# Twelve more k pairs in seven block products in the two SwiGLU FFNs of a decoder trunk

## The chip, the cores and the metric

The kernel runs on one core of one Trainium2 chip. The metric is the device time of one execution in microseconds (us). Beside it there is a trace of one profiled execution, with the start and the length of each instruction on each engine: TensorE (PE, with its weight loads as PEld), VectorE (DVE), ScalarE (ACT), GpSimd (POOL), and SyncE (SP), which issues most of the DMAs.

## The reference

The reference is a trunk of two decoder layers, each a mixer and a SwiGLU FFN, on 256 tokens of width 2048 in float32. Everything is matrix products over large weights with small work between them. The change is in the FFN:

```python
def swiglu(xn, w_gate, w_up, w_down):
    return (jax.nn.silu(xn @ w_gate) * (xn @ w_up)) @ w_down
...
        h = h + swiglu(rms_norm(h, norm_ffn[layer]), w_gate[layer], w_up[layer], w_down[layer])
```

w_gate and w_up are 2048 x 5632, w_down is 5632 x 2048, for each of the two layers.

## The kernel before, in words

**Split products.** TensorE takes fp32 data here in the reduced type fp32r. So each operand is split in two such parts, hi and lo: ScalarE casts raw to hi (L177), VectorE writes lo = raw - hi (L178). A product is then three matmuls, hi by hi, hi by lo and lo by hi (`three`, L508 to L511), each 128x128 by 128x512. Activations are split once and stay in SBUF: xh and xl for the input of gate and up, mh and ml for the input of down. Weights are split as they arrive, 512 KB at a time: a tile `raw` of 128x2x512, which is two k tiles of 128 rows (a k pair) by 512 columns. There are six buffers each for a weight's hi and lo and four for raw.

**Plain pairs and mixed pairs.** `pair_group` (L516 and on) computes a 2x2 arrangement of results at once: two weight matrices (gate and up columns, or two column blocks of down) by two blocks of 128 tokens (t0, t1). For a k pair it has two ways. A *plain* pair does all eight block products, 8 x 3 = 24 matmuls, into four PSUM banks (`plain`, "acc" in the trace); it needs two 1024-wide splits. A *mixed* pair does the 2x2 block product by the Strassen-Winograd scheme with seven products, 7 x 3 = 21 matmuls: four of them go to four further banks (`prods`), three to the plain ones. For that VectorE makes four 512-wide differences of the raw weights (L568 to L571), two of them in a tile t4 and two in place in raw. ScalarE and VectorE split these as ht and lt (two buffers each, so one mixed pair's worth), and the up weight's second k tile as a 512-wide hi and lo. Of the activations, four sums per pair are needed, made ahead of time by `sums_of` (L253 to L266) and kept split in sx (gate and up) and sd (down).

**Closing a group.** `combine` (L523 to L531) copies the first product bank to a tile c on ScalarE and adds the others on VectorE, with four 512-wide additions. Then gate/up groups add the four plain banks (L619), apply Silu (L621), multiply by the up half and the norm factor (L623), and turn the result to [hidden, token] by DMA transposes. The turned tile is joined and split into mh and ml (and the sums for down) some pairs later, inside the next group (`join`, after the position MID = 6, or MID_DOWN = 5 in a down group). Down groups add c to the residual h with four 512-wide additions (L708) and then the plain banks (`add_out`, L353).

**The order of the work.** An FFN has eleven gate/up groups of 512 hidden columns, in three parts PARTS = (0, 3, 7, 11): groups 0 to 2, 3 to 6, and 7 to 10. After each part follow two down groups over that part's hidden rows (12, 16 and 16 k tiles; in layer 1's last part the second is done with plain products alone). Which pairs are mixed, and in what order, is a list of (kind, pair) with kind 1 for mixed:

```python
ORDER = ((0, 0), (1, 1), (0, 2), (1, 3), (0, 4), (1, 5), (0, 6), (0, 7))
DOWN = {
    6: ((0, 0), (1, 1), (0, 2), (1, 3), (0, 4), (0, 5)),
    8: ((0, 0), (1, 1), (0, 2), (1, 3), (0, 4), (1, 5), (0, 6), (0, 7)),
}
```

So a group over eight pairs has three mixed ones: 5 x 24 + 3 x 21 = 183 matmuls. The banks alternate: a group's products use the four banks that held the plain results of the group before it. Each engine's instruction order is fixed when the kernel is built, by a scheduler that interleaves the matmuls of neighbouring pairs; each engine then runs its list in order and waits on semaphores. Weight loads are issued from SP.

Of the kernel before, what the change touches and what calls it, by code (L numbers as in the profile page):

```python
# [17 lines left out]
P = 128  # L18
D = 2048
S = 256  # L20
# [15 lines left out]
ORDER = ((0, 0), (1, 1), (0, 2), (1, 3), (0, 4), (1, 5), (0, 6), (0, 7))  # L36
DOWN = {
# [35 lines left out]
def trunk(  # L73
# [179 lines left out]
    def sums_of(pool, sh, sl, copies, full=None, tags=("tmp", "tmp"), bufs=None, box=None):  # L253
# [9 lines left out]
        nc.vector.tensor_tensor(out=s[:, 1, :], in0=s[:, 0, :], in1=full[:, 0, 0, :], op=ALU.subtract)  # L263
        nc.vector.tensor_tensor(out=s[:, 2, :], in0=full[:, 0, 0, :], in1=full[:, 0, 1, :], op=ALU.subtract)
        nc.vector.tensor_tensor(out=s[:, 3, :], in0=full[:, 1, 0, :], in1=s[:, 1, :], op=ALU.subtract)
        split_plain(sh, sl, s)  # L266

    def split_scaled(idx, n, extra=None, joined=None):
        for half in range(2):
# [13 lines left out]
            if extra is not None and pair in mixed_of(ORDER):  # L283
                sh, sl, pool = extra
                j = mixed_of(ORDER).index(pair)

                def copies(full):
                    for i in range(2):
                        g = gT[:, idx * KT + 2 * pair + i : idx * KT + 2 * pair + i + 1]
                        nc.scalar.mul(full[:, i, :], pt[:, i, :, :].rearrange("p t q -> p (t q)"), g)  # L290

                sums_of(pool, sh[:, j, :, :], sl[:, j, :, :], copies)
# [200 lines left out]
    def out_proj(w, idx, key, extra):  # L493
        last, rest = KT - 4, []
        for n0 in (0, 2):
# [3 lines left out]
            for i in range(2):  # L499
# [3 lines left out]
                    (LATER[n0 + i], split_turned(idx, n0 + i, *scrap(extra[2], n0 + i), extra))  # L503
                )
                square_sum(key, n0 + i)
        return rest

# [8 lines left out]
    def pair_group(fp, par, lhs, sums, mats, order, todo=(), halves=None, inner=None, raws=None):  # L516
        plain = [[bank(par, "acc") for _ in range(NT)] for _ in range(2)]
        todo = list(todo)
# [13 lines left out]
        for pos, (kind, pair) in enumerate(order):  # L532
# [4 lines left out]
            if not kind:  # L537
# [4 lines left out]
                for m, (w, c0) in enumerate(mats):  # L542
                    hi, lo = load_chunk(w, k0, c0, NB)
                    run_due(todo, pos)
                    for i, t in walk:
# [4 lines left out]
                            pos == 0 and i == 0, last and i == CK - 1,  # L550
# [38 lines left out]
            three(plain[0][0], xb[:, t0], lb[:, t0], hg[:, 1, :], lg[:, 1, :], False, False)  # L589
            three(plain[1][0], sh[:, 3, :], sl[:, 3, :], hu[:, 1, :], lu[:, 1, :], False, False)  # L590
            three(prods[1], sh[:, 0, :], sl[:, 0, :], ht[0], lt[0], first, last)
            three(prods[2], sh[:, 2, :], sl[:, 2, :], ht[1], lt[1], first, last)
            three(prods[3], sh[:, 1, :], sl[:, 1, :], ht[2], lt[2], first, last)
            three(plain[0][1], xb[:, t1], lb[:, t1], ht[3], lt[3], False, False)
# [4 lines left out]
    def ffn(layer, fp, sx, sd, key, todo, idx_next=None, key_next=None, finish=None):  # L599
        r = rstd(key)  # L600

        def sums_x(pair):
            j = mixed_of(ORDER).index(pair)
            return sx[0][:, j, :, :], sx[1][:, j, :, :]

        for g0, g1 in zip(PARTS, PARTS[1:]):
            end = g1 == PARTS[-1]
            nk = 4 * (g1 - g0)
            order = DOWN[nk // 2]
            for g in range(g0, g1):  # L610
                par = (g1 - 1 - g) % 2
                plain, c = pair_group(
                    fp, par, x_of, sums_x, [(w_gate[layer], g * NB), (w_up[layer], g * NB)], ORDER, todo
                )
                todo = []
                for m in range(2):
                    for t in range(NT):
                        o = c[:, 2 * m + t, :]
                        nc.vector.tensor_tensor(out=o, in0=plain[m][t], in1=o, op=ALU.add)  # L619
                for t in range(NT):  # L620
                    nc.scalar.activation(c[:, t, :], c[:, t, :], AF.Silu, scale=r[:, t : t + 1])  # L621
                for t in range(NT):
                    nc.vector.scalar_tensor_tensor(  # L623
                        out=c[:, t, :], in0=c[:, 2 + t, :], scalar=r[:, t : t + 1], in1=c[:, t, :], op0=ALU.mult, op1=ALU.mult
# [24 lines left out]
                def join(c=c, turned=turned, g=g, g0=g0, order=order):  # L649
# [8 lines left out]
                    for half in range(2):  # L658
                        pair = 2 * (g - g0) + half
                        if pair in mixed_of(order):  # L660
# [3 lines left out]
                                sd[0][:, j, :, :],  # L664
                                sd[1][:, j, :, :],
# [6 lines left out]
            def sums_d(pair, order=order):  # L672
                j = mixed_of(order).index(pair)
                return sd[0][:, j, :, :], sd[1][:, j, :, :]
# [16 lines left out]
            for n0 in (0, 2):  # L691
# [20 lines left out]
    def close_layer(layer, w_out, idx, key, **rest):  # L712
        with tc.tile_pool(name=f"fp{layer}", bufs=2) as fp:
# [3 lines left out]
            todo = out_proj(w_out, idx, key, (*sx, fp))  # L717
            sd = [fp.tile([P, nd, 4, P], F32R, tag=f"sd{i}", name=f"sd{i}", bufs=1) for i in range(2)]
            ffn(layer, fp, sx, sd, key, todo, **rest)
# [22 lines left out]
    with tc.tile_pool(name="ev", bufs=1) as ev:  # L742
# [223 lines left out]
        with tc.tile_pool(name="mp", bufs=1) as mp:  # L966
            def sums_m(pair):
                j = mixed_of(MIXQ).index(pair)
                return sx[0][:, j, :, :], sx[1][:, j, :, :]
# [129 lines left out]
    with tc.tile_pool(name="od", bufs=1) as od:  # L1099
# [65 lines left out]
        def sums_x(pair):  # L1165
            j = mixed_of(MIX).index(pair)
            return sx[0][:, j, :, :], sx[1][:, j, :, :]
# [154 lines left out]
```

## Time and profile before

| | us |
|---|---|
| median of 3 runs | 2077.48 |
| lowest and highest | 2077.07, 2077.85 |
| span of the profiled execution | 2076.6 |
| FFN of layer 0 (in that span) | 322.9 to 1009.3 |
| FFN of layer 1 | 1380.7 to 2066.9 |
| TensorE busy | 2066.4 |
| VectorE busy | 1824.5 |
| ScalarE busy | 1374.7 |
| GpSimd busy | 41.7 |

The profiled execution's own time is that of its span, from its first to its last instruction; the median of the runs is 0.9 us above it. Rows of an engine's busy time count the instructions' durations, merged where they overlap. A matmul's duration (0.39 us in the trace) includes the pipeline behind it, so that the distance of two starts, and not the duration, tells what one costs. In the views of the profile, each row names the engine, the line of the kernel before, the operation, and "output <- inputs" by the program's names; "x4" counts instructions taken together.

### The profile page before, as it was taken

The numbers are of one execution on the slowest core, as the hardware profiler recorded it, in microseconds if no ns is written. First come the engines' busy times: TensorE is split into PE (matmuls) and PEld (weight loads), VectorE is DVE, ScalarE is ACT, GpSimd is POOL, SyncE is SP. The second block draws the span as 40 slices with busy tenths as digits, with TensorE's granted clock in tenths as the row PEclk, the third lists the DMA queues.
The fourth block names the chain that finished last, engine by engine and source line by source line (L and its number), as shares of the span: only waits on it lengthen the run. The fifth ranks groups of instructions, "written<-read, shape, count | busy, mean of one in ns | idle before, by whom it ended". The sixth has DMA issues, their size and how long they took to land.

```text
span 2076.6 us, 26994 instructions
## 1 busy us (share of the span) xinstructions
PE 2066.4 (100%) x9473; PEld 1715.0 (83%) x9473; DVE 1824.5 (88%) x2410; ACT 1374.7 (66%) x1736; POOL 41.7 (2%) x66
## 2 busy tenths in 40 slices
PE   9999999999999999999999999999999999999998
PEld 7878888888888888888888888888888888888887
DVE  6788769999999999999899778689999999999994
ACT  6777678765676656667676776687655667456763
POOL 1010000000000000000000001000000000000000
PEclk9999999999999999999999999999999999999999
DMA  8566577666566666666576866586665667666764
GB/s 292 172 213 188 190 247 236 203 217 206 189 230 223 205 210 205 220 212 204 185 215 204 235 193 184 156 283 220 206 205 200 213 206 234 203 202 213 220 197 138
DMA packets 309575, 434.87 MB, mean 209 GB/s; under 512 B 106412, under 2 KB 114624, under 8 KB 309312
## 3 DMA queue, kind: packets, MB, share of 16 engines
q1 hardware_dynamic: 307088, 426.27, 65.1%
q0 software_dynamic: 1632, 5.80, 0.8%
q8 instruction: 74, 1.21, 0.2%
q10 hardware_dynamic: 720, 1.09, 0.2%
q14 instruction: 61, 0.50, 0.1%
HBM read 408.68 MB, written 2.12 MB: 198 GB/s over the span
## 4 chain that ended last, share of the span: by engine, by line
PE 97%; DVE 1%; ACT 1%; DMA 1%; issue 1%; SPq 0%; POOLq 0%; POOL 0%; ACTq 0%; DVEq 0%
PE acc L510 21%; PE acc L509 21%; PE acc L511 21%; PE acc L213 5%; PE acc L212 5%; PE acc L214 5%; PE prod L509 5%; PE prod L510 5%; PE prod L511 5%; PE p L369 1%; PE po L470 1%; DMA raw<-in_w_in_odd_dram 0%; ACT s L403 0%; PE po L471 0%; DVE lo L178 0%
## 5 line engine op out<-in xcount | busy, mean ns | idle before, releaser
L177 ACT CAST hi<-raw 128x1024 fp32r<-128x1024 f32 (+3 forms) x656 | 664.8, 1028 | 440.2 <-PE acc L511 269.1
L178 DVE TENSOR_TENSOR lo<-raw,hi 128x1024 fp32r<-128x1024 f32 (+3 forms) x656 | 772.8, 1192 | 146.3 <-ACT hi L177 143.5
L510 PE MATMUL acc<-lo,xh 128*128 128x512 f32 x1254 | 488.6, 390 | 0.0
L509 PE MATMUL acc<-hi,xh 128*128 128x512 f32 x1254 | 485.9, 390 | 0.5 <-ACT hi L177 0.5
L511 PE MATMUL acc<-hi,xl 128*128 128x512 f32 x1254 | 484.8, 389 | 0.0
L510 PEld LDWEIGHTS acc<-lo,xh 128*128 128x128 f32 x1254 | 235.4, 188 | 49.4 <-DVE lo L178 0.6
L509 PEld LDWEIGHTS acc<-hi,xh 128*128 128x128 f32 x1254 | 235.2, 188 | 49.5 <-ACT hi L177 0.7
L511 PEld LDWEIGHTS acc<-hi,xl 128*128 128x128 f32 x1254 | 235.4, 188 | 48.8
L510 PE MATMUL acc<-lo,mh 128*128 128x512 f32 x437 | 169.7, 389 | 0.0
L511 PE MATMUL acc<-hi,ml 128*128 128x512 f32 x437 | 168.4, 389 | 0.0
L509 PE MATMUL acc<-hi,mh 128*128 128x512 f32 x437 | 167.9, 389 | 0.0
L339 ACT CAST hi<-raw 128x512 fp32r<-128x512 f32 x109 | 67.6, 620 | 89.4 <-PE acc L511 80.5
L213 PE MATMUL acc<-lo,mh 128*128 128x512 f32 (+1 forms) x322 | 126.3, 392 | 0.0
L212 PE MATMUL acc<-hi,mh 128*128 128x512 f32 (+1 forms) x322 | 125.8, 391 | 0.0
L214 PE MATMUL acc<-hi,ml 128*128 128x512 f32 (+1 forms) x322 | 123.7, 391 | 0.0
L340 DVE TENSOR_TENSOR lt<-t,ht 128x1024 fp32r<-128x1024 f32 x95 | 115.8, 1219 | 5.2 <-ACT ht L339 5.1
L339 ACT CAST ht<-t 128x1024 fp32r<-128x1024 f32 x95 | 99.9, 1051 | 30.7 <-PE prod L511 28.8
L339 ACT CAST ht<-raw 128x1024 fp32r<-128x1024 f32 x95 | 99.7, 1050 | 29.7 <-PE acc L511 15.0
L340 DVE TENSOR_TENSOR lt<-raw,ht 128x1024 fp32r<-128x1024 f32 x95 | 115.7, 1218 | 1.8 <-ACT ht L339 1.8
L213 PE MATMUL acc<-lo,xh 128*128 128x512 f32 (+3 forms) x288 | 99.8, 348 | 0.2 <-DVE lo L178 0.2
L214 PE MATMUL acc<-hi,xl 128*128 128x512 f32 (+3 forms) x288 | 98.1, 344 | 0.0
L212 PE MATMUL acc<-hi,xh 128*128 128x512 f32 (+3 forms) x288 | 95.9, 347 | 0.3
(363 smaller groups left out, 3448.0 us busy)
## 6 DMA issues: line engine op xcount, KB each, us to landing
raw<-in_w_gate_dram SPq DMA_DIRECT2D x176, 512.0 KB, 4.5
raw<-in_w_up_dram SPq DMA_DIRECT2D x176, 512.0 KB, 4.6
raw<-in_w_down_dram SPq DMA_DIRECT2D x176, 512.0 KB, 5.1
raw<-in_w_in_odd_dram SPq DMA_DIRECT2D x88, 512.0 KB, 4.9
raw<-in_w_in_even_dram SPq DMA_DIRECT2D x51, 512.0 KB, 5.0
raw<-in_w_out_even_dram SPq DMA_DIRECT2D x32, 512.0 KB, 5.1
raw<-in_w_out_odd_dram SPq DMA_DIRECT2D x32, 512.0 KB, 4.8
hr<-in_w_in_even_dram SPq DMA_DIRECT2D x12, 512.0 KB, 4.6
```

The costliest lines, as they stand in the source:

```text
L177: latest[0] = nc.scalar.copy(hi[:, k, 0:n], raw[:, k, 0:n])
L178: nc.vector.tensor_tensor(out=lo[:, k, 0:n], in0=raw[:, k, 0:n], in1=hi[:, k, 0:n].bitcast(F32), op=ALU.subtract)
L212: nc.tensor.matmul(o, ah[:, ts], hi, start=(k == 0), stop=False)
L213: nc.tensor.matmul(o, ah[:, ts], lo, start=False, stop=False)
L214: nc.tensor.matmul(o, al[:, ts], hi, start=False, stop=(k == k_all - 1 and cs.stop == n))
L339: nc.scalar.copy(dst_h, src)
L340: nc.vector.tensor_tensor(out=dst_l, in0=src, in1=dst_h.bitcast(F32), op=ALU.subtract)
L369: nc.tensor.matmul(pq[j % 2][:, j // 2, :], q_of(j, b), k_of(j)[:, 0:cols], start=True, stop=True)
L470: nc.tensor.matmul(po, v_of(j, 0), tt[:, j, 0:2, :].rearrange("p c q -> p (c q)"), start=True, stop=False)
L509: nc.tensor.matmul(o, ah, hi, start=start, stop=False)
L510: nc.tensor.matmul(o, ah, lo, start=False, stop=False)
L511: nc.tensor.matmul(o, al, hi, start=False, stop=stop)
```

## The change

Four gate/up groups of each layer (1, 4, 6, 8) and both down groups of the middle part take four mixed pairs instead of three, in a new order that starts with a mixed pair and alternates. The added mixed pair is number 7.

- Its four sums need room. Of x, three go to the t1 halves of xh and xl at the k tiles 2, 6 and 10, which nobody reads (a mixed pair's first k tile is read in its t0 half alone), and the fourth to a new tile x4. Of the middle part's hidden activations all four go to the t1 halves of mh and ml at the k tiles 2, 6, 10 and 14.
- The first matmul into a bank sets its start flag through a helper `fresh`, since a group can now begin with a mixed pair.
- `combine` does the last two additions as one of 128x2x512 (with the up and gate columns of c in a new order), and the additions to h in a down group become two of 128x1024, in every group of the FFN.
- The scratch space of the software DMA queue (POOL's) goes from 4096 to 2048, which makes SBUF room for x4.

In the built program there are 36 matmuls fewer, and VectorE has 2449 rows where it had 2410, ScalarE 1662 where it had 1628; POOL and SP have as many as before.

```diff
+HEAVY = ((1, 1), (0, 0), (1, 3), (0, 2), (1, 5), (0, 4), (1, 7), (0, 6))
+FOURTH = 7
+DENSE = (1, 4, 6, 8)
+DEEP = (3,)
...
-        split_plain(sh, sl, s)
+        if x4 is None:
+            split_plain(sh, sl, s)
+        else:
+            split_plain(sh, sl, s[:, 0:3, :])
+            split_plain(x4[:, 0, :], x4[:, 1, :], s[:, 3, :])
...
-            if extra is not None and pair in mixed_of(ORDER):
-                sh, sl, pool = extra
-                j = mixed_of(ORDER).index(pair)
+            if extra is not None and (pair in mixed_of(ORDER) or pair == FOURTH):
+                sh, sl, x4, pool = extra
...
+                if pair == FOURTH:
+                    sums_of(pool, rooms(xh), rooms(xl), copies, x4=x4)
+                else:
+                    j = mixed_of(ORDER).index(pair)
+                    sums_of(pool, sh[:, j, :, :], sl[:, j, :, :], copies)
...
+    def rooms(m):
+        return m[:, 2:11:4, P:S]
...
+        begun = set()
+
+        def fresh(*at):
+            known = at in begun
+            begun.add(at)
+            return not known
...
+            if halves is None:
+                nc.vector.tensor_tensor(out=c[:, 1, :], in0=prods[3], in1=c[:, 0, :], op=ALU.add)
+                nc.vector.tensor_tensor(out=c[:, 2, :], in0=prods[2], in1=c[:, 1, :], op=ALU.add)
+                nc.vector.tensor_tensor(
+                    out=c[:, 1:4:2, :],
+                    in0=prods[1].rearrange("p (a n) -> p a n", a=1).broadcast_to([P, 2, NB]),
+                    in1=c[:, 1:3, :],
+                    op=ALU.add,
+                )
+                return c
...
-                            pos == 0 and i == 0, last and i == CK - 1,
+                            fresh(m, t), last and i == CK - 1,
...
         def sums_x(pair):
+            if pair == FOURTH:
+                return [[m[:, k, P:S] for k in (2, 6, 10)] + [x4[:, a, :]] for a, m in enumerate((xh, xl))]
...
-            order = DOWN[nk // 2]
+            order = HEAVY if g0 in DEEP else DOWN[nk // 2]
             for g in range(g0, g1):
                 par = (g1 - 1 - g) % 2
                 plain, c = pair_group(
-                    fp, par, x_of, sums_x, [(w_gate[layer], g * NB), (w_up[layer], g * NB)], ORDER, todo
+                    fp,
+                    par,
+                    x_of,
+                    sums_x,
+                    [(w_gate[layer], g * NB), (w_up[layer], g * NB)],
+                    HEAVY if g in DENSE else ORDER,
+                    todo,
                 )
...
             def sums_d(pair, order=order):
+                if pair == FOURTH:
+                    return [[m[:, k, P:S] for k in (2, 6, 10, 14)] for m in (mh, ml)]
...
-                for m in range(2):
-                    for t in range(NT):
-                        o = h[:, t, (n0 + m) * NB : (n0 + m + 1) * NB]
-                        nc.vector.tensor_tensor(out=o, in0=c[:, 2 * m + t, :], in1=o, op=ALU.add)
+                for t in range(NT):
+                    o = h[:, t, n0 * NB : (n0 + 2) * NB]
+                    nc.vector.tensor_tensor(
+                        out=o, in0=c[:, 2 * t : 2 * t + 2, :].rearrange("p a n -> p (a n)"), in1=o, op=ALU.add
+                    )
...
-    nc = _bacc.Bacc("TRN2", target_bir_lowering=False, num_devices=1, dynamic_dma_scratch_size=4096)
+    nc = _bacc.Bacc("TRN2", target_bir_lowering=False, num_devices=1, dynamic_dma_scratch_size=2048)
```

More of the change, by code (lines that the diff above doesn't have):

```diff
@@ L506, in out_proj, with four @@
         return rest
+    def four(s, j):
+        return [s[:, j, e, :] for e in range(4)]
+    def rooms(m):
+        return m[:, 2:11:4, P:S]
     def three(o, ah, al, hi, lo, start, stop):
@@ L588, in pair_group @@
             three(prods[0], xa[:, t0], la[:, t0], hg[:, 0, :], lg[:, 0, :], first, last)
[L589 to L594, printed above, removed]
+            three(plain[0][0], xb[:, t0], lb[:, t0], hg[:, 1, :], lg[:, 1, :], fresh(0, 0), False)
+            three(plain[1][0], sh[3], sl[3], hu[:, 1, :], lu[:, 1, :], fresh(1, 0), False)
+            three(prods[1], sh[0], sl[0], ht[0], lt[0], first, last)
+            three(prods[2], sh[2], sl[2], ht[1], lt[1], first, last)
+            three(prods[3], sh[1], sl[1], ht[2], lt[2], first, last)
+            three(plain[0][1], xb[:, t1], lb[:, t1], ht[3], lt[3], fresh(0, 1), False)
         if inner is None:
@@ L663, in join @@
                                 fp,
-                                sd[0][:, j, :, :],
-                                sd[1][:, j, :, :],
+                                *[sums_m[:, j, :, :] if pair != FOURTH else m[:, 2:15:4, P:S] for sums_m, m in zip(sd, (mh, ml))],
                                 None,
```

31 lines of the change are left out of this document (18 added, 13 removed).

## The prediction, made before the changed kernel ran

> **What bounds the kernel now.** I read the profile in this order: busy shares, then stretches of the FFN as a table by stage, then the groups of VectorE's instructions in those stretches, then waits, then the timeline around one block-product pair. The first page says that TensorE is never without work, and that VectorE is the next engine:
>
> ```profile
> span 2076.6 us, 26994 instructions
> PE 2066.4 (100%) x9473; PEld 1715.0 (83%) x9473; DVE 1824.5 (88%) x2410; ACT 1374.7 (66%) x1736; POOL 41.7 (2%) x66
> ```
>
> 88% is a mean over stages. The change sits in the two FFNs, so I cut the trace there. The first fence holds both FFNs whole, the second four stretches of 41.5 us, one group each, of layer 0's middle part: gate/up groups 4, 5 and 6 and the first down group:
>
> ```profile
> 322.90:1009.30 686.40, 686.40 (x3037) 568.41 (x3036) 647.55 (x807) 448.85 (x508) 0.69 (x1) 1.00 0.65 208
> 1380.70:2066.90 686.20, 686.20 (x3033) 568.17 (x3032) 629.93 (x781) 433.64 (x484) 1.79 (x3) 1.00 0.64 205
> ```
>
> ```profile
> 552.20:593.70 41.50, 41.50 (x185) 34.37 (x184) 39.74 (x52) 28.30 (x31) 0.00 (x0) 1.00 0.66 218
> 593.70:635.20 41.50, 41.50 (x185) 34.37 (x184) 39.98 (x52) 28.68 (x32) 0.00 (x0) 1.00 0.66 217
> 635.20:676.70 41.50, 41.50 (x185) 34.37 (x184) 39.74 (x51) 28.47 (x31) 0.00 (x0) 1.00 0.67 215
> 676.70:718.20 41.50, 41.50 (x185) 34.37 (x184) 39.88 (x49) 26.91 (x28) 0.00 (x0) 1.00 0.67 216
> ```
>
> The columns are the stretch, its length, then busy time with count for PE, weight loads, DVE, ACT and POOL, the granted clock, and the DMA share with GB/s. PE is busy through all of both FFNs (686.40 of 686.40), so every matmul taken out is worth its full pitch, as long as nothing else becomes late. But DVE is busy for 39.7 to 40.0 of each 41.5 us. Only some 1.5 to 2.3 us per group are free there. DMA (0.65) and ACT (28 of 41.5) have room.
>
> A matmul's pitch, and DVE's and ACT's own spacing, come from starts that follow each other:
>
> ```profile
> 621.25 0.39 PE L510 MATMUL acc<-lo,sx 128*128 128x512 f32 x1
> 621.48 0.39 PE L511 MATMUL acc<-hi,sx 128*128 128x512 f32 x1
> 621.71 0.62 PE L509 MATMUL prod<-ht,sx 128*128 128x512 f32 x2
> 622.16 0.39 PE L510 MATMUL prod<-lt,sx 128*128 128x512 f32 x1
> ```
>
> ```profile
> 616.68 0.29 DVE L263 TENSOR_TENSOR s<-s,c 128x128 f32<-128x128 f32 x1
> 616.88 1.22 DVE L340 TENSOR_TENSOR lt<-t,ht 128x1024 fp32r<-128x1024 f32 x1
> ...
> 619.35 0.69 DVE L568 TENSOR_TENSOR t<-raw 128x512 f32<-128x512 f32 x1
> 619.95 0.69 DVE L569 TENSOR_TENSOR t<-raw 128x512 f32<-128x512 f32 x1
> 620.55 1.22 DVE L340 TENSOR_TENSOR lt<-raw,ht 128x1024 fp32r<-128x1024 f32 x1
> ...
> 622.29 4.63 DVE L178 TENSOR_TENSOR lo<-raw,hi 128x1024 fp32r<-128x1024 f32 x4
> 626.83 1.22 DVE L340 TENSOR_TENSOR lt<-t,ht 128x1024 fp32r<-128x1024 f32 x1
> ...
> 630.71 0.68 DVE L528 TENSOR_TENSOR c<-prod,c 128x512 f32<-128x512 f32 x1
> 631.31 0.68 DVE L529 TENSOR_TENSOR c<-prod,c 128x512 f32<-128x512 f32 x1
> 631.91 0.68 DVE L340 TENSOR_TENSOR lo<-raw,hi 128x512 fp32r<-128x512 f32 x1
> ```
>
> Four matmuls lie between 621.25 and 622.16: 0.2267 us each. Four 1024-wide DVE operations take (626.83 - 622.29)/4 = 1.135 us each, 512-wide ones 0.600 (619.35, 619.95, 620.55; from PSUM too: 630.71, 631.31, 631.91), 128-wide ones 0.20 (616.68 to 616.88). The durations are 0.085 longer than these intervals because the instructions overlap; I add intervals. The 512-wide scalar_tensor_tensor gets 0.746 - 0.085 = 0.66 (groups of DVE's instructions from 510.8 to 676.7 us; busy time, mean ns, idle time before):
>
> ```profile
> L178 DVE TENSOR_TENSOR lo<-raw,hi 128x1024 fp32r<-128x1024 f32 x52 | 62.5, 1220 | 5.1 <-ACT hi L177 5.0
> L340 DVE TENSOR_TENSOR lt<-t,ht 128x1024 fp32r<-128x1024 f32 x12 | 14.6, 1221 | 1.5 <-ACT ht L339 1.4
> L623 DVE SCALAR_TENSOR_TENSOR c<-c,r 128x512 f32<-128x512 f32 x6 | 4.2, 746 | 0.0
> ```
>
> **The change, part by part.** *TensorE.* A k pair taken as seven products issues 21 matmuls, as eight products 24. Twelve more pairs (two layers, each four gate/up groups and two down groups) remove 36 matmuls: 36 x 0.2267 = **-8.16 us**. The built order has exactly 36 fewer, and the order outside the FFNs is unchanged.
>
> *VectorE, one pair.* A plain pair is two 1024-wide subtractions (2.27 us). A mixed pair is three of them and five 512-wide operations: 3 x 1.135 + 5 x 0.600 = 6.40. So each turned pair adds **4.13 us on DVE and removes 0.68 us from PE**.
>
> *VectorE, one group.* Before, a gate/up group is 5 x 2.27 + 3 x 6.40 = 30.55 of pairs, 4 x 0.6 to combine, 4 x 0.6 for L619, 2 x 0.66 for L623, and 2.5 for the join of the turned tile (1.135 + four 128-wide + one 512-wide): 39.2 us against 183 x 0.2267 = 41.49 on PE. That agrees with the rows of 39.7 to 40.0 (whose ends count overlap). Spare: 2.3 us. The two merges are worth little: one 1024-wide instead of two 512-wide saves 1.200 - 1.135 = 0.065 us. After:
> - a dense gate/up group: 4 x 2.27 + 4 x 6.40 + 2.33 + 2.4 + 1.32 + 2.53 = 43.3 against 180 x 0.2267 = 40.81: **short by 2.5**;
> - the first down group of the middle part: 34.7 + 2.33 + 2.27 (h) + 2.4 (L353) + 2.53 = 44.2: short by 3.4;
> - the second (no join): 41.7: short by 0.9.
>
> Groups 1 and 4 stand between groups with 2.3 us to spare. But group 6 and both down groups follow each other: 2.5 + 3.4 + 0.9 = 6.8 us short in a row; then comes group 7, light, and group 8, short again.
>
> *Page against row.* The Trainium skill, in "VectorE: DVE Perf Modes", section "The TRN2 errata", gives the fp32 tensor_tensor add as (N+151)/0.96 ns: 0.691 us for 512, 1.224 for 1024. The trace agrees on single durations (0.69, 1.22). Adding such durations over a group of before (20 x 1.224 + 24 x 0.691 + 2 x 0.746 + 4 x 0.285) would make 43.7 us, and PE would stall by 2 us in each group; the rows show no stall, so the intervals decide.
>
> *How far DVE is ahead.* A shortage costs nothing until DVE's lead over PE is used up. The lead is limited by buffers: ht and lt have two tiles each, so the next pair's ht cast on ACT waits until PE has read the last one. What it is now, at a second mixed pair of a group:
>
> ```profile
> 615.40 1.05 ACT L339 CAST ht<-t 128x1024 fp32r<-128x1024 f32 x1
> ```
>
> The cast ends at 616.45, the lt subtraction quoted above at 616.88 + 1.22 = 618.10, and PE reads lt at 622.16: 4.1 us ahead. I take 5.0, somewhat in favour of the change.
>
> *The running sum.* In the built order of the changed kernel I start at the lt of group 6's second mixed pair with a lead of 5.0 and add up both engines to the L353 addition that frees the first bank for the second down group's products. DVE, after that lt: 41 operations of 1024, 51 of 512, two of L623, eight of 128: 41 x 1.135 + 51 x 0.6 + 2 x 0.66 + 8 x 0.2 = 80.1. PE, between the two readers: 311 matmuls, 70.5. So DVE ends 80.1 - 70.5 - 5.0 = **4.6 us** late, in each layer (layer 1 has the same sequence).
>
> This supposes that DVE never waits on the way. It must: the built order puts the lt products of group 6's second and third mixed pairs almost side by side on PE (only 12 matmuls between the last reader of the second's ht and the first reader of the third's lt). The third's ht cast can't start until that reader is done, so DVE, 5 us ahead, does its four subtractions (2.4) and then idles: 5.0 + 0.2 + 1.05 - 2.4, some 3.5 us. After it, the lead is 12 x 0.2267 - 1.05 - 1.22 = 0.4. From there to the same L353 addition DVE has 40 x 1.135 + 47 x 0.6 + 2 x 0.66 + 8 x 0.2 = 76.5 and PE 299 matmuls, 67.8: 76.5 - 67.8 - 0.4 = **8.3 us** late.
>
> Group 8: from its first mixed pair to its last DVE has 28.0 us (15 x 1.135 + 17 x 0.6 + 4 x 0.2) against 98 matmuls (22.2) and a lead of 5.0: 0.8, and up to 4.9 if DVE idles on ht as above. Groups 1 and 4: 0 to 1.2, with their neighbours' slack.
>
> *The small parts.* Three more sums of x, for pair 7 (four 128-wide, the splits, four scalings on ACT): +1.5 us on DVE ahead of group 0, covered by its 2.3 of slack; 0 to 1.5 per layer if not. ACT's extra work, two 1024 casts of 1.05 less half a cast, is 1.5 us per pair and goes into its 13 us of idle time per group. Fourth sums in unread halves need no new wait on a reader. No DMA is added on SP. The software queue's smaller ring touches POOL alone, outside the FFN (below).
>
> *Sum.* Per layer the least is 4.6 + 0.8 = 5.4, with idling 8.3 + 0.8 to 4.9 + 0 to 1.2 = 9.1 to 14.4. Both layers: 10.8 at least, 18 to 29 with idling. Less 8.16: +2.6 at least, **+10 to +21** with idling. I take the lower part, +13, because the ends of the idling sums use the lead at its smallest at each place. The profiled execution is 2076.6 and the runs are 0.9 above it (median 2077.5); the difference is added to the latter: **2090 us**.
>
> **Rivals.**
> 1. *The cover holds.* Over a whole FFN, DVE goes from 647.55 to 647.55 + 6 x 4.13 - 16 x 0.065 - 11 x 0.065 + 1.5, some 672, still below PE's 686.4 - 4.1 = 682.3. If DVE were free to run far ahead, its slack of 35 us would absorb everything: 2077.5 - 8.2 = **2069**. For it: six weight buffers (three pairs) let DVE split plain chunks earlier, and ACT mostly waits for PE (waits from 510.8 to 759.6 us: total, times, longest):
>
> ```profile
> ACT hi L177 <- PE acc L511: 51.7, 35, 4.2
> DVE lo L178 <- ACT hi L177: 8.0, 15, 1.1
> ```
>
> Against it: the same row says that the lead is already at its cap, so slack can't be saved up beyond it, and 6.8 us short in a row are more than 5. It decides from a lead of about 10 us at group 6.
> 2. *The shortage without idling*: +2.6, **2080**. For it: DVE's order has other splits to put into a gap; against it, that order is fixed when the kernel is built.
> 3. *Worse hand-overs.* With a mixed pair first, the products need the banks of the group before at once, where a plain pair's 24 matmuls (5.4 us) stood between. If each of the six dense groups per layer waits 1 to 2 us for L619 or L353: 2090 + 12 to 24 us, **above 2102**.
> 4. *The POOL queue.* With half the ring its DMAs wait for each other. The row that shows POOL waiting for such loads:
>
> ```profile
> POOL cb L1151 <- DMA cb<-scratch: 20.7, 4, 6.7
> ```
>
> Doubled, it would be 20.7 us more on POOL, of which nothing ended on PE before; at the outside +20, **2110**, with PE idle outside the FFNs.
> 5. *The change doesn't do what it says*: the built order has the 36 matmuls fewer and DVE's 48 further 512-wide subtractions, so I give this nothing.
>
> **How the numbers follow.** Forecast (shortage with idling, 2084 to 2102): 0.62. Rival 2 (2078 to 2083): 0.17. Rival 1 (2067 to 2073): 0.09. Rival 3: 0.08. Rival 4: 0.04. The range is 2078 to 2102: it leaves out rival 1, rival 3 and most of rival 4, about 0.2. A difference of 0.2% (4.2 us) is about what a measurement of this kernel can tell from none: faster 0.09, same 0.14 (rival 2 below 2081.6), slower 0.77.
>
> **What would show it.** In the changed profile: PE waits in the FFN for DVE's lt and lo and for c or h, where there were none; those waits concentrated from group 6's third mixed pair to the second down group, 6 to 9 us per layer, and a few us in group 8; DVE near 100% from group 6 to the down groups and a DVE wait on ACT's ht of about 3 us in group 6; 36 matmuls fewer at an unchanged pitch of 0.2267; no change outside the FFNs. I am wrong if PE stays gapless (rival 1), if the gaps are at the first products of the dense groups and wait for bank releases (rival 3), or if gaps appear outside the FFNs (rival 4).

## The result

The changed kernel takes **2151.0 us** (median of 4 runs, 2147.8 to 2151.9), the kernel before 2077.3, measured beside it: a ratio of 1.035, 95% interval 1.0337 to 1.0366. The forecast was 2090, with a range up to 2102. The sign was right, the size was not: +74 us, where +13 had been worked out. The profiled execution has a span of 2146.1.

First the busy times of the changed kernel, from the head of its profile:

```profile
span 2146.1 us, 26989 instructions
PE 2086.6 (97%) x9437; PEld 1707.8 (80%) x9437; DVE 1872.6 (87%) x2449; ACT 1394.3 (65%) x1770; POOL 43.8 (2%) x66
```

TensorE has 36 records fewer, as the change says, and VectorE 48 us more work (1824.5 to 1872.6). Yet VectorE's share fell, from 88% to 87%. It isn't busier; the span grew by more than its work. The stretches that answer to the two FFN rows of before, in the same columns:

```profile
323.00:1043.90 720.90, 697.58 (x3020) 564.99 (x3018) 669.27 (x825) 457.41 (x523) 0.69 (x1) 0.99 0.64 198
```

```profile
1419.30:2136.00 716.70, 695.49 (x3014) 562.62 (x3013) 653.26 (x803) 443.98 (x502) 1.75 (x3) 1.00 0.64 197
```

The FFNs grew by 34.5 us (686.4 to 720.9) and 30.5 us (686.2 to 716.7). Another 4.0 us lie between them, from the end of the one to the start of the other (1009.3 to 1380.7 before: 371.4; 1043.9 to 1419.3: 375.4). That is 69.0 of the 69.5 us by which the span grew, so nothing is lost elsewhere. TensorE now waits. The waits of the whole span, of which before had none over 1.2 us:

```profile
PE prod L526 <- ACT ht L350: 15.8, 13, 3.1
PE prod L527 <- DVE lt L351: 8.3, 9, 1.6
PE acc L527 <- DVE lo L182: 4.3, 6, 1.3
PE acc L526 <- ACT hi L181: 4.1, 6, 1.1
PE pt L283 <- DVE h L364: 3.7, 1, 3.7
```

The two largest are for the cast ht of a mixed pair and the split lt behind it, 24.1 of the 36.2 us shown. And VectorE, which was to be the bound, waits itself in the FFN of layer 0 (total, times, longest); the kernel before, then the changed one:

```profile
DVE lo L178 <- ACT hi L177: 22.3, 40, 1.5
DVE lt L340 <- ACT ht L339: 2.6, 5, 1.4
```

```profile
DVE lt L351 <- ACT ht L350: 15.5, 14, 3.3
DVE lo L182 <- ACT hi L181: 9.8, 16, 3.2
DVE lo L351 <- ACT hi L350: 7.9, 7, 1.8
DVE c L551 <- PE prod L528: 6.4, 3, 4.0
DVE t L602 <- DMA raw<-in_w_down_dram: 3.3, 2, 2.0
DVE t L602 <- DMA raw<-in_w_up_dram: 3.1, 4, 1.3
```

The waits for ht went from 2.6 to 15.5 us, and waits for weights appear where there were none. The waits for hi (L177, now L182) went the other way, from 22.3 to 9.8 us.

**By stretch.** The groups' limits follow from counting matmuls from the FFN's first one. From group 6 to the end of the middle part's down groups, before and in the change:

```profile
635.25:759.65 124.40, 124.40 (x550) 103.00 (x550) 118.99 (x147) 77.14 (x82) 0.00 (x0) 1.00 0.66 212
```

```profile
642.45:782.40 139.95, 128.97 (x542) 99.63 (x541) 126.26 (x155) 80.71 (x90) 0.00 (x0) 1.00 0.60 184
```

This stretch should be 2.0 us shorter (nine matmuls fewer) and is 15.6 us longer, so 17.6 us are lost. The whole FFN of layer 0, in us, with 0.68 us (three matmuls) for each dense group added to the growth:

| | before | change | lost | forecast |
|---|---|---|---|---|
| group 0 | 41.5 | 41.5 | 0.0 | 0 to 1.5 |
| groups 1 and 2, first part's down groups | 146.5 | 154.3 | 8.5 | 0 to 1.2, with group 4 |
| groups 3 to 5 | 124.5 | 123.8 | 0.0 | as above |
| group 6, middle part's down groups | 124.4 | 140.0 | 17.6 | 4.6 to 8.3 |
| groups 7 to 9 | 124.5 | 129.5 | 5.7 | 0.8 to 4.9 |
| group 10, last part's down groups | 125.2 | 132.0 | 6.8 | none |

The series that the forecast had worked out lost twice its upper figure, and more than half of the loss lies outside it.

**One place closely: group 6.** The timeline of ScalarE, then that of VectorE, in the changed kernel:

```profile
660.20 1.05 ACT L350 CAST ht<-t 128x1024 fp32r<-128x1024 f32 x1 [1.62 <-PE prod L528]
661.16 1.05 ACT L350 CAST ht<-raw 128x1024 fp32r<-128x1024 f32 x1
662.11 1.99 ACT L693 COPY c<-c 128x1024 uint16<-128x1024 uint16 x2
667.06 1.35 ACT L700 COPY c<-turned 128x1024 uint16<-128x1024 uint16 x1 [2.96 <-DMA turned<-c]
668.36 1.05 ACT L350 CAST ht<-t 128x1024 fp32r<-128x1024 f32 x1
```

```profile
665.49 0.69 DVE L605 TENSOR_TENSOR raw<-raw 128x512 f32<-128x512 f32 x1
669.45 1.23 DVE L351 TENSOR_TENSOR lt<-t,ht 128x1024 fp32r<-128x1024 f32 x1 [3.27 <-ACT ht L350]
671.01 0.29 DVE L266 TENSOR_TENSOR s<-c 128x128 f32<-128x128 f32 x1 [0.33 <-ACT c L700]
671.22 0.28 DVE L268 TENSOR_TENSOR s<-c 128x128 f32<-128x128 f32 x1
672.84 0.69 DVE L602 TENSOR_TENSOR t<-raw 128x512 f32<-128x512 f32 x1 [1.34 <-DMA raw<-in_w_up_dram]
```

ScalarE's join of group 5 (L700) waits 3 us for the turned tiles, and the next ht cast stands behind it in ScalarE's list. But that cast could hardly have come sooner. It overwrites one of the two ht tiles, and TensorE was still reading it; the last matmul that does so is this one:

```profile
667.94 0.39 PE L528 MATMUL prod<-ht,sx 128*128 128x512 f32 x1
```

It ends at 668.33, and the cast starts at 668.36. So VectorE's wait of 3.3 us for that cast is the one that the prediction had at this place, "some 3.5 us", and the join's wait lies inside it. What the prediction didn't have is the 1.3 us more for a weight. In the kernel before the same two copies came together, with no wait, 7.3 us after the 16-bit copies that feed the transposes:

```profile
644.25 1.99 ACT L646 COPY c<-c 128x1024 uint16<-128x1024 uint16 x2
...
653.50 2.58 ACT L653 COPY c<-turned 128x1024 uint16<-128x1024 uint16 x2
```

The chain of waits of the changed kernel from 662 to 690 us (start, length, piece) shows a third party, SyncE's queue:

```profile
662.21 1.90 ACT c L693 x2
664.11 0.27 SPq L695
664.42 1.26 SPq L695
...
665.78 1.21 SPq L695
...
667.03 1.26 SPq L695
...
668.40 4.36 DMA raw<-in_w_up_dram
...
672.84 0.69 DVE t L602
```

L695 issues the transposes, four of them, one after another on the queue that issues the weight loads too. The next weight load leaves behind them, 4.3 us after the copies that start them (664.11 to 668.40), and takes 4.4 us; VectorE stands at L602 until it lands. TensorE's two largest gaps in this group follow from it: 0.8 us at 673.45, for a cast of that weight, and 1.6 us at 675.53, for the lt that stands behind L602 in VectorE's list.

### The profile page after: what moved, and what is told of

Read it like the earlier page. It is cut to its first block, busy times and chain, and to the rows that moved or that the text cites. A ratio compares the mean times of both kernels' runs of the same rounds, so it can differ in the third digit from the quotient of the medians.

```text
span 2146.1 us, 26989 instructions
## 1 busy us (share of the span) xinstructions
PE 2086.6 (97%) x9437; PEld 1707.8 (80%) x9437; DVE 1872.6 (87%) x2449; ACT 1394.3 (65%) x1770; POOL 43.8 (2%) x66
## 4 chain that ended last, share of the span: by engine, by line
PE 75%; DVE 10%; DMA 5%; issue 4%; ACT 4%; SPq 2%; ACTq 0%; POOLq 0%; DVEq 0%; POOL 0%
PE acc L526 15%; PE acc L527 15%; PE acc L528 15%; PE acc L217 5%; PE acc L216 5%; PE acc L218 5%; PE prod L526 4%; PE prod L528 4%; PE prod L527 4%; DVE lo L182 3%; DMA raw<-in_w_down_dram 3%; DVE lt L351 2%; SPq L695 1%; DMA raw<-in_w_up_dram 1%; ACT hi L181 1%
## 5 line engine op out<-in xcount | busy, mean ns | idle before, releaser
L181 ACT CAST hi<-raw 128x1024 fp32r<-128x1024 f32 (+2 forms) x644 | 649.5, 1026 | 372.2 <-PE acc L528 220.7
L182 DVE TENSOR_TENSOR lo<-raw,hi 128x1024 fp32r<-128x1024 f32 (+2 forms) x644 | 756.5, 1189 | 119.6 <-ACT hi L181 116.6
L527 PE MATMUL acc<-lo,xh 128*128 128x512 f32 x1198 | 467.8, 390 | 0.0
L528 PE MATMUL acc<-hi,xl 128*128 128x512 f32 x1198 | 464.2, 390 | 0.0
L526 PE MATMUL acc<-hi,xh 128*128 128x512 f32 x1198 | 460.5, 391 | 3.8 <-ACT hi L181 2.3
L350 ACT CAST ht<-t 128x1024 fp32r<-128x1024 f32 x107 | 112.4, 1051 | 108.8 <-PE prod L528 78.7
L351 DVE TENSOR_TENSOR lt<-t,ht 128x1024 fp32r<-128x1024 f32 x107 | 130.4, 1219 | 33.7 <-ACT ht L350 32.7
L351 DVE TENSOR_TENSOR lt<-raw,ht 128x1024 fp32r<-128x1024 f32 x107 | 130.2, 1216 | 0.8 <-ACT ht L350 0.4
L217 PE MATMUL acc<-lo,mh 128*128 128x512 f32 (+1 forms) x322 | 126.3, 392 | 0.0
L350 ACT CAST ht<-raw 128x1024 fp32r<-128x1024 f32 x107 | 112.1, 1048 | 8.3 <-DVE raw L605 6.2
L526 PEld LDWEIGHTS acc<-hi,mh 128*128 128x128 f32 x413 | 78.4, 190 | 26.6 <-ACT hi L181 4.0
```

The costliest lines, as they stand in the source:

```text
L181: latest[0] = nc.scalar.copy(hi[:, k, 0:n], raw[:, k, 0:n])
L182: nc.vector.tensor_tensor(out=lo[:, k, 0:n], in0=raw[:, k, 0:n], in1=hi[:, k, 0:n].bitcast(F32), op=ALU.subtract)
L217: nc.tensor.matmul(o, ah[:, ts], lo, start=False, stop=False)
L350: nc.scalar.copy(dst_h, src)
L351: nc.vector.tensor_tensor(out=dst_l, in0=src, in1=dst_h.bitcast(F32), op=ALU.subtract)
L526: nc.tensor.matmul(o, ah, hi, start=start, stop=False)
```

## The experiments

Each is the changed kernel with the edit shown, unless it says otherwise. Three theories were held against each other first: A, VectorE's own work; B, waits that pass from queue to queue in the built order; C, the merged additions.

**Parts of the change: e1 to e3, and its order: e4.**

```diff
e1  DENSE = ()               DEEP = ()
e2  DENSE = (1, 4, 6, 8)     DEEP = ()
e3  DENSE = ()               DEEP = (3,)
e4  HEAVY = ((0, 0), (1, 1), (0, 2), (1, 3), (0, 4), (1, 5), (1, 7), (0, 6))
```

> No group has a fourth mixed pair (DENSE and DEEP empty); the merged additions in c and h, the sums of pair 7 and the smaller queue space stay, and TensorE has the matmul count of before. Three theories are held against each other. Theory A (throughput: VectorE simply has too much to do in the dense groups): 2076 to 2079, no TensorE gaps in the FFNs. Theory B (order: with the dense groups the built order closes the group before late, and waits pass from one engine's queue to the next): the same, 2076 to 2079. Theory C (the merged additions and the new layout of c hold the down groups of the first and last part up, where gaps of 5 to 8 us per layer were seen although they got no fourth pair): about 2077 + 2 x (5 to 8) + 2 x (5 to 7) = 2097 to 2107.

> Only the gate/up groups 1, 4, 6 and 8 have a fourth mixed pair (8 groups, 24 matmuls fewer, -5.4 us); the down groups are as before. Theory A: each dense group is short by 2.5 us and stands beside groups with 2.3 us to spare and a lead of some 5 us, so nothing or little is lost: 2072 to 2078. Theory B: the gaps at groups 1 and 8 and a part of those at group 6 stay, and so do the gaps in the down groups of the first and last part: 2077 - 5.4 + 2 x (4 + 5 + 6 + 6 + 7) = about 2120, at least 2095.

> Only the two down groups of the middle part have a fourth mixed pair (4 groups, 12 matmuls fewer, -2.7 us). Theory A: short by 3.4 + 0.9 us in a row with a lead of about 5: 2074 to 2080. Theory B: a part of the gaps between group 6 and the second down group stays, 5 to 12 us per layer, and nothing elsewhere: 2085 to 2099.

> The whole change, but the dense order begins with a plain pair and has the mixed pairs 1, 3, 5, 7 behind it: (0,0), (1,1), (0,2), (1,3), (0,4), (1,5), (1,7), (0,6). Work on each engine is unchanged to the instruction, only its order moves. Theory A: as the change, 2140 to 2155. Theory B: the plain pair in front lets the group before close in time, and much of the loss goes: 2090 to 2125.

Measured: e1 2081.1 (ratio 1.0015, 1.0006 to 1.0025), e2 2114.2 (1.018), e3 2090.6 (1.006), e4 2147.3 (1.034), before 2077.8. C falls: the merges, together with pair 7's sums and the smaller ring, cost 3.3 us, not 20. A, as I had sized it, falls with e2: e2, with four dense groups per layer, takes 36.4 us more than before, where A allowed none. e2 and e3 also show that the parts don't add up: over e1 they lose 33.1 and 9.5, together 42.6; the whole change loses 69.9 over e1. B falls in one form with e4, since a plain pair in front changes nothing.

**Single dense groups: e9, e10.**

```diff
e9   DENSE = (4, 8)   DEEP = ()   the 512-wide additions of before
e10  DENSE = (6,)     DEEP = ()
```

> Only gate/up groups 4 and 8 have a fourth pair (4 groups, 12 matmuls fewer, -2.7 us), down groups as before, 512-wide additions as before. In the run with all four dense gate/up groups TensorE had no gap in groups 4 and 8 of either layer; both stand inside a part, with light groups on each side. Theory A (a single dense group's 2.5 us fit into the lead and its neighbours' slack): 2074 to 2077, the only version so far that would beat the kernel before. Theory B (any dense group disturbs the built order): 2080 to 2095.

> Only gate/up group 6 of each layer has a fourth pair (6 matmuls fewer, -1.4 us); the merged additions stay (2081 without the pair). Group 6 is the last of its part: its neighbours are the down groups. Theory A: one dense group is absorbed, 2079 to 2083. Theory B: the gaps of about 10 us per layer that the run with four dense groups had between 670 and 730 us are group 6's own: 2095 to 2105.

e9: 2079.3 (ratio 1.0007, 0.9999 to 1.0016), no change that can be told. e10: 2084.8 (1.0034), 3.7 us over e1. Group 6 alone doesn't make the 10 us of gaps per layer that e2 had around it. A single dense group can be carried, but the 2.7 us of matmuls that e9 takes out bring nothing either.

**VectorE's added work, and the transposes: e5, e6, e11, e13.** e5 leaves pair 7's four subtractions out; e6 the FFN's DMA transposes, so that down reads unturned hidden values (ten groups of each layer are turned by DMA; the last group of the first part is turned on TensorE, L679 of the changed kernel, and stays so); e11 does both; e13 is the kernel before with e6's edit.

```diff
e5   bare = pair == FOURTH and halves is None
     t4 = ra if halves else rb if bare else fp.tile(...)
     if not bare:
         (L602 to L605)
e6  -nc.sync.dma_start_transpose(turned[b][:, :, t, :], flat[:, b, t, :])
    -nc.scalar.copy(cb[:, :, b], turned[b].rearrange("p k t q -> p (k t q)"))
    +nc.scalar.copy(cb[:, :, b], flat[:, b, :, :].rearrange("p t n -> p (t n)"))
```

> The whole change, but pair 7's four subtractions (L602 to L605) are left out: its ht and lt are made from the raw weights, so the products of that pair are not those of the scheme. That takes 4 x 0.6 = 2.4 us off VectorE in each of the 12 added pairs, and leaves their matmuls, casts and splits. Theory A (VectorE is short of time in the dense groups, by 2.5, 3.4 and 0.9 us): nearly all the shortage is gone, and with the 2 to 8 us that the merges cost 2073 to 2085. Theory B (the built order makes waits pass between ScalarE, VectorE and the DMA queue, whatever VectorE's load): ht has the same two buffers and the join stands in the same place, so half or more of the loss stays, 2105 to 2140.

> The whole change, but the DMA transposes of the FFN's hidden tiles are left out: the join copies the tile back as it lies, not turned, so that down is computed from hidden values in the wrong places. VectorE's and TensorE's work is the same; ScalarE has nothing to wait for between its two pairs of 16-bit copies. Theory A: as the change, 2140 to 2155. Theory B with the join as its place (ScalarE waited 3 us for turned tiles in group 6, with the next pair's ht cast queued behind, and VectorE then 3.3 us for ht): 2100 to 2130.

> The whole change without pair 7's four subtractions and without the DMA transposes (both as before in these runs: products and hidden values are not those of the reference). Each alone took 28 to 29 us off. If VectorE's load and ScalarE's wait for turned tiles are separate causes they add up: 2151 - 57 = 2090 to 2098, and what is left above 2069 are the merges and the ht buffers. If they are two ends of one queue (either alone removes the same gaps): 2112 to 2122.

> The kernel before without the DMA transposes (down is computed from unturned hidden values). TensorE has no gap there, so whatever the transposes do to ScalarE is hidden: 2076 to 2079. If it gets faster by several us, the 28 us that the changed kernel gained without them are not the dense groups' own.

Measured: e5 2121.8 (1.021), e6 2123.3 (1.022), e11 2091.7 (1.006), e13 2077.1 against 2078.0 (0.9997, 0.9988 to 1.0006). So 29.2 us go with the subtractions (12 x 2.4 = 28.8 us of VectorE's time, one for one), 27.7 with the transposes, 59.3 with both: two parts that add up, and the transposes cost nothing in the kernel before. e5 does one thing more than relieve VectorE: without the differences the casts to ht need not wait for them. How much of its 29.2 us is due to that was not separated. The FFN of layer 0, in the same columns as above, from 322.9 us to its last matmul, in before, the change, e5, e6 and e11:

```profile
322.90:1009.60 686.70, 686.70 (x3040) 568.58 (x3038) 647.85 (x808) 448.85 (x508) 0.69 (x1) 1.00 0.65 207
```

```profile
322.90:1044.10 721.20, 697.87 (x3021) 565.05 (x3019) 669.57 (x825) 457.70 (x523) 0.69 (x1) 0.99 0.64 198
```

```profile
322.90:1031.20 708.30, 691.50 (x3018) 566.42 (x3016) 655.92 (x800) 456.94 (x523) 0.69 (x1) 0.99 0.66 202
```

```profile
322.90:1030.40 707.50, 692.40 (x3018) 563.07 (x3016) 668.89 (x824) 457.08 (x522) 0.69 (x1) 1.00 0.62 194
```

```profile
322.90:1016.30 693.40, 687.43 (x3018) 564.64 (x3016) 654.84 (x800) 457.76 (x523) 0.69 (x1) 1.00 0.63 198
```

Length less VectorE's busy time is VectorE's idle time:

| | FFN of layer 0 | VectorE busy | idle |
|---|---|---|---|
| before | 686.7 | 647.9 | 38.9 |
| change | 721.2 | 669.6 | 51.6 |
| e5, no subtractions | 708.3 | 655.9 | 52.4 |
| e6, no transposes | 707.5 | 668.9 | 38.6 |
| e11, neither | 693.4 | 654.8 | 38.6 |

Here the loss comes apart. The subtractions move the busy time and leave the idle time; the transposes move the idle time and leave the busy time. And where the transposes are gone, VectorE is as idle as before, 38.6 us. The slack that was to absorb the added work was never used.

**The path of the transposes: e7, e15, e17.** e7 has MID = 7 and MID_DOWN = 7; in the first down group of the middle part pair 7, and of the last part pair 6, then read their hidden values from before the join, so these waits are left out. e15 has MID = 7 alone. e17 has two tiles c instead of one, and five hi and lo buffers.

```diff
e7   MID = 7   MID_DOWN = 7
e15  MID = 7
e17 -c = fp.tile([P, 4, NB], F32, tag="c", name="c", bufs=1)
    +c = fp.tile([P, 4, NB], F32, tag="c", name="c", bufs=1 if halves else 2)
    -wp = ctx.enter_context(tc.tile_pool(name="wp", bufs=6))
    +wp = ctx.enter_context(tc.tile_pool(name="wp", bufs=5))
```

> The whole change, with the join due at position 7 instead of 6 (gate/up) and 5 (down). Theory A: as the change, 2140 to 2155. Theory B with the join as its place: the copies stand later in ScalarE's queue, the transposes have landed, and 10 to 30 us go, 2120 to 2140; more is lost, up to 2170, where the down group then waits for the hidden tile.

> The whole change with the join of a gate/up group due at position 7 instead of 6; in the down groups it stays at 5, and all values are those of the change. If ScalarE's wait for turned tiles costs because the next mixed pair's ht cast is queued behind it, moving the join behind the last mixed pair gains a part of the 28 us that the transposes cost: 2125 to 2145. If the built order only shuffles: 2145 to 2160.

> The whole change with two buffers for the tile c instead of one, paid for with five instead of six hi and lo buffers (which cost the kernel before 16 us in e14, together with a third ht buffer that it can't use much). A group's products can't be added up before the last group's c has been turned, joined and split. If that cycle through the one c (with the transposes in it) is how the transposes cost 28 us: 2167 - 28 or more, at most 2140. If c's cycle has room: 2150 to 2170.

Measured: e7 2131.1 (1.026), e15 2144.3 (1.032), e17 2149.4 (1.035). ScalarE's waits for turned tiles, in the change and in e15:

```profile
ACT c L700 <- DMA turned<-c: 28.9, 19, 3.9
```

```profile
ACT c L700 <- DMA turned<-c: 6.8, 10, 1.8
```

22 us of this wait went, and 7 us of the time. So ScalarE's wait is not the main way in which the transposes cost. e7 gains 19.9 us with every transpose still issued, but it also leaves two waits out, and in its middle part it has a stretch of its own: from 721.7 to 738.9 us TensorE's granted clock is 0.50, with waits of up to 2.7 us in between, and 24 matmuls run in these 17.2 us, where 76 would fit at the usual pitch. So its gain can't be put down to the place of the join alone. e17 can't be read well, since its five buffers have a price of their own (e14).

The chain quoted above shows a weight load queued behind the transposes on SyncE. As the main way this was not tested by itself: the transposes were not moved to another queue. The waits speak against it: over the whole span VectorE waits 10.7 us for weights at L602 in the change, and still 10.4 us without the transposes (e6). What goes with the transposes is TensorE's wait for ht, in the change 15.8 us (18.6 in e15), while its wait for c's addition L552 grows from 1.4 to 7.9 us. The wait for ht in e6:

```profile
PE prod L526 <- ACT ht L350: 2.7, 5, 0.8
```

**The two ht buffers: e12, e14, e16.** Three ht and three lt tiles, with five hi and lo buffers instead of six; e14 is the kernel before with that edit, e16 is e11 with it.

```diff
-hs = fp.tile([P, 2, NB], F32R, tag="ht", name="ht")
+hs = fp.tile([P, 2, NB], F32R, tag="ht", name="ht", bufs=3)
-wp = ctx.enter_context(tc.tile_pool(name="wp", bufs=6))
+wp = ctx.enter_context(tc.tile_pool(name="wp", bufs=5))
```

> The whole change with three buffers each for ht and lt instead of two, paid for with five instead of six buffers for a weight's hi and lo. If the loop of ht (TensorE reads the last pair, then ScalarE casts, then VectorE splits) is what holds VectorE back, as its 33 us of waiting for ht suggest: 2090 to 2125. If not: 2145 to 2165, with the smaller lookahead on top.

> The kernel before with three buffers for ht and lt and five for a weight's hi and lo. It prices the fifth buffer: from the trace of the changed kernel with the same buffers some 7 us per mixer are lost outside the FFNs, so 2085 to 2095. If so the third ht buffer is worth more than the 14 us seen: about 22 to 30.

> The whole change without pair 7's four subtractions, without the transposes, and with three ht and lt and five hi and lo buffers. If the three causes add up and nothing else is left: 2091.7 less 14, about 2074 to 2082. If the third ht buffer only helps where VectorE is short, it gains nothing here: 2088 to 2100.

Measured: e12 2136.9 (1.029), e14 2094.3 (1.008), e16 2113.5 (1.017). In the kernel before, the edit costs 16.4 us; in the change it gains 14.1. VectorE's waits for ht over the whole span, in the change and in e12:

```profile
DVE lt L351 <- ACT ht L350: 33.1, 27, 3.3
```

```profile
DVE lt L351 <- ACT ht L350: 4.7, 6, 2.1
```

So the two ht buffers do hold VectorE back in the change. But in e16, with VectorE relieved and the transposes gone, the edit costs 21.8 us over e11: there the edit gains nothing, so the third buffer is no third part that adds to the two. That it gets back some of what the same lateness costs is how I read it, and isn't shown.

**The merges: e8, e18.** The 512-wide additions of before, in the change (e8) and in e11 (e18).

```diff
-nc.vector.tensor_tensor(out=c[:, 1:4:2, :], in0=prods[1]..., in1=c[:, 1:3, :], op=ALU.add)
+nc.vector.tensor_tensor(out=c[:, 3, :], in0=prods[1], in1=c[:, 2, :], op=ALU.add)
+nc.vector.tensor_tensor(out=c[:, 1, :], in0=prods[1], in1=c[:, 1, :], op=ALU.add)
...
+                for m in range(2):
                     for t in range(NT):
-                        o = h[:, t, n0 * NB : (n0 + 2) * NB]
+                        o = h[:, t, (n0 + m) * NB : (n0 + m + 1) * NB]
```

> The whole change, but with the 512-wide additions of before in combine and into h. The merges alone cost 3.3 us. Theory A: they cost the same here, or save 0.065 us x 55 of VectorE: 2145 to 2155. Theory B (any move in the built order shifts the chains): 2120 to 2150, the end of layer 0 without its gap of 3.7 us.

> As e11 (without pair 7's four subtractions and without the transposes, 2091.7), with the 512-wide additions of before. If the rest of the loss is the merges and the gap of 3.7 us at the end of layer 0: 2080 to 2087. If the merges are not in it: 2089 to 2094.

Measured: e8 2143.8 (1.032), e18 2100.8 (1.011). Taking the merges back gains 7.2 us in the one and loses 9.1 in the other. Any edit moves the whole built order, and differences of this size between two builds can't be put down to the edit. That holds for the 6.7 us of e15 too.

## Why the prediction was wrong

**Right.** The matmuls went (36), at an unchanged pitch. VectorE's busy time in layer 0's FFN was put at 672 us and is 669. VectorE's wait for ht at group 6's third mixed pair was put at 3.5 us and is 3.3. TensorE waits for lt and lo, as said, though longest in total for ht itself. Nothing happened outside the FFNs but for one gap. POOL's smaller ring (rival 4) shows nothing: the wait that it was to double went from 20.7 to 22.3 us, and e1, which has the ring, is 3.3 us above before. The cover (rival 1) didn't hold. Rival 3, waits for banks at the first products of dense groups, had little in it: TensorE's waits for c's copy and additions are 4.7 us in all over the span, and e4, with the plain pair in front, is as slow.

**The step that failed: the running sum, and in it VectorE's idle time.** I let VectorE wait once per layer, 3.5 us in group 6, and counted every light group's 2.3 us and a lead of 5.0 as usable, so that a layer would lose 9 to 14 us, up to 4.9 of it in group 8. Measured, a layer loses 34.5 + 4.1 = 38.6 us of TensorE's time in the first FFN (its growth and the 18 matmuls that went). By the rows of the FFN, VectorE works 21.7 us more and is idle 12.8 us more: the 34.5 us of growth. To meet the forecast, its idle time had to fall from 39 to some 24 us. VectorE was to be near 100% busy from group 6 to the down groups; it is busy for 126.3 of 140.0 us there, 90%, where it had 119.0 of 124.4, 96%. The one wait that the sum allowed came as worked out (3.3 us of group 6); in that stretch VectorE is idle for 13.7 us. I read this as a loss in ordered queues and not in engine time: each of PE, ACT, DVE and SP runs a fixed list, and a late instruction holds up all that stands behind it. e5 gives the price, with the reservation made there: 29.2 us of time for 28.8 us of VectorE's work, and 31.6 us for the same work between e6 and e11, though VectorE is idle for 5 to 7% of the FFN.

**The term that was missing: the transposes.** 27.7 us of the 73.7. The sum treated the join as VectorE's 2.5 us and left out its chain: closing additions, L665, the 16-bit copies, four transposes on SyncE at 1.25 us each, the join's copies. In the kernel before that chain ends with time to spare. In the change, the closing of the group before comes later (in group 6, L665's second one ends at 660.8, 18 us after that group's first matmul; before, group 6's first matmul is at 635.3 and L623's second one ends at 642.1, 7 us), and its transposes fall where the next mixed pair's weight is due. I had written that no DMA is added on SP. None is; those already there came at another time.

**What grew with it.** Neighbouring dense groups cost more than their sum: group 6 alone 5.1 us (3.7 over e1, and the 1.4 of its matmuls), the whole change 78 us over e1 less its matmuls. The forecast had seen group 6 and the down groups as one series; the trace shows gaps in the down groups of the first and of the last part too, which take no fourth pair (TensorE's ht wait of 3.1 us, the longest, is in the last part's first down group of layer 0). Groups 1 and 8, with the groups behind them, lost 8.5 and 5.7 us, while group 4 lost nothing; why these differ stays open.

**Figures of the working that don't come out.** The wait of "some 3.5" is 3.85 by its own terms, the 4.9 us of group 8 are not worked out, and the slack of rival 1, given as 35 us, is 38.9 by the rows. None of them changes the account.

**The gap at the end of layer 0** (3.7 us, L283 for L364) is not in any step. There the merged additions into h come as whole 1024-wide operations ahead of L364, but they don't explain it: e1, which has them, has 1.7 us of it, e8 and e18 1.9 without merges, e3 3.7. It isn't settled what sets its size.

**What stays open.** e11 is still 10.6 us above e1, and 18.8 above e1 less the 8.2 us of matmuls. Single waits there are at most 3.7 us and of many kinds. By which path the transposes cost (SyncE's queue, ScalarE's list, contention of their packets) wasn't separated; e15 and the waits in e6 only make the first two, each by itself, unlikely as the main one.

## What to carry to other kernels

When every engine runs a fixed list, the spare time of a nearly full engine is not a reserve: add up its work and its present idle time, and ask which of its waits would have to vanish for the new work to fit. Follow each chain that returns to the engine (closing, copies, transposes, the queue that issues loads) and see how much time it has to spare; the transposes, which cost nothing before (e13), cost 27.7 us in the change. Here the second engine was busy for 94% of the FFN (647.9 of 686.7 us), and a trade of 4.1 us on it for 0.7 us on the first gained nothing when made twice per layer (e9), and lost when made six times.

## What the runs showed of the hardware

Some short gaps of TensorE are followed by a few us at about half rate. Around one gap in the changed kernel the granted clock (third from the right) falls to 0.57:

```profile
401.00:404.00 3.00, 0.96 (x5) 0.50 (x4) 3.00 (x4) 2.51 (x3) 0.00 (x0) 1.00 0.99 361
404.00:408.00 4.00, 4.00 (x11) 3.13 (x12) 4.00 (x7) 1.10 (x2) 0.00 (x0) 0.57 0.28 51
```

TensorE is idle for 2.04 us, and from 403.86 to 407.27 us the matmuls start 0.42 to 0.43 us apart instead of 0.23:

```profile
403.86 0.62 PE L526 MATMUL prod<-ht,xh 128*128 128x512 f32 x1 [2.04 <-ACT ht L350]
404.28 0.63 PE L526 MATMUL acc<-ht,xh 128*128 128x512 f32 x1
404.71 0.63 PE L527 MATMUL prod<-lt,xh 128*128 128x512 f32 x1
```

A longer gap, with 2.41 us of idle time up to 1500.50, is followed by no such stretch; the clock stays at 1.00:

```profile
1500.50:1504.00 3.50, 3.19 (x12) 2.01 (x12) 3.50 (x5) 1.10 (x2) 0.00 (x0) 1.00 0.15 56
```

So the length of a gap alone doesn't decide. The Trainium skill, in "TensorE: Matmul & The Clock Gate", section "What's actually happening", puts the fall to half clock after an idle window of about 3.4 us that runs freely; here 2.04 us of idle time were enough in one place, and 2.41 us were not in another. Counted over both FFNs, 27 matmuls stand at the wider spacing, 27 x 0.2 = 5.4 us: a small part of the loss, but one that comes on top of some of the longer waits.
